# Products of ones on TensorE ahead of transposes, Gram products and the last branch's last blocks

## The chip, the cores and the metric

The kernel runs on one core of one Trainium2 chip. The metric is the device time of one execution in microseconds (us); several executions give a median. TensorE (PE in the profile) multiplies matrices into PSUM, VectorE (DVE) and ScalarE (ACT) do elementwise work, GpSimd (POOL) some of it, and SyncE (SP) issues most loads. The profile shows for every stretch the clock that TensorE was granted, as a share of full speed: 1.0 is 2.4 GHz, 0.5 is 1.2 GHz.

## The reference

One transformer block in float32, batch 1, 1024 tokens, width 1024. Two branches, an RWKV7 recurrence and a differential attention, are gated, mixed and projected; then come a mixture of 32 experts and a gated per-layer input. What the change is about is the first half:

```python
h = rms_norm(x, norm_mix[l])
proj = h @ w_in[l]
p_rwkv = proj[..., :RWKV_COLS]
p_diff = proj[..., RWKV_COLS:RWKV_COLS + DIFF_COLS]
g_rwkv, g_diff = jnp.split(proj[..., RWKV_COLS + DIFF_COLS:], 2, axis=-1)
o_rwkv = rwkv7_branch(p_rwkv, ...)      # 8 heads of 64, a scan over the tokens
o_diff = diff_attention_branch(p_diff, ...)
mixed = (jax.nn.sigmoid(g_rwkv) * (o_rwkv @ w_branch_rwkv[l])
         + jax.nn.sigmoid(g_diff) * (o_diff @ w_branch_diff[l]))
x = x + mixed @ w_out[l]
x = x + hierarchical_moe(rms_norm(x, norm_ffn[l]), ...)   # 4 groups of 8 experts, top 2
ple_gate = jax.nn.sigmoid(rms_norm(x, norm_ple[l]) @ w_ple_gate[l])
x = x + ple_gate * (p[l] @ w_ple_proj[l])
```

## The kernel before

Every large product is made of three (`mm3`, lines 69 to 71): both factors are split into a high and a low part by `split` (ACT makes the high part on line 76, DVE the low part on line 77), and three products of 512 or 256 columns are summed in PSUM.

The program runs in stages. From 0 to about 480 us: the input projection and the attention. From 480 to 703 us: the gate columns of the projection (`gates`, PSUM tile `pg8`, shown as pg) and, woven between them, `rwkv_prep` for the eight chunks of 128 tokens, c0 to c7. A chunk computes decays and keys on DVE, ACT and POOL, and then TensorE transposes 128x128 blocks into the PSUM tiles ptr (line 331): first eight of `al` and `rh` (shown as ee and ei), whose copies make AR, then eight of `be` and `ka` (shown as be and iv), whose copies make BK, in halves of four. AR, BK, LT and the rows are written to DRAM. `rwkv_inv` inverts the 32x32 blocks of four chunks in 30 serial steps on DVE (lines 400 and 402).

From 703 to 990 us: the recurrence, again chunk after chunk. `rwkv_gram` loads a chunk and makes Gram products per head (tile pG, lines 377 and 378, masked into G by DVE); `rwkv_levels` loads the inverted blocks Xd (line 414, four loads a chunk), has DVE transpose them (XT) and doubles them on TensorE (tiles pQ); `rwkv_step` makes pR, pS and pD, `rwkv_out` makes pY. Between these steps fillers run: `branch_diff` for both halves of the tokens, then one product for the per-layer input (ppp), then the RWKV branch for the first half. `branch_diff` loads four blocks of 128 rows of the attention's output (orow, line 779), transposes each (tpd, line 782), splits it (odh on ACT, odl on DVE), and calls `branch`, which makes eight blocks j of 12 products each (tile pbr) against a branch weight (braw, split to bwh and bwl) and multiplies each by a gate (bgt) on DVE (line 766 for the attention, 769 with tile btm for RWKV).

From 990 to 1030 us: the last branch, `branch(0, 1, ...)`, eight blocks of 12 products, beside the load and split of the output weight (woh, wol). Then output projection and routing up to 1165 us, the experts to 1770 us, and the last gate.

A scheduler sets the order: the program is written as generators that hand over in turns, and the framework's scheduler, with a simulated timeline, orders the instructions on each engine from that, under the dependences, the pools' buffers and the order that `issue_after` adds. An engine then works strictly through its list.

Of the kernel before, what the change touches and what calls it, by code (L numbers as in the profile page):

```python
# [22 lines left out]
F32 = mybir.dt.float32  # L23
# [29 lines left out]
class Kern:  # L53
# [13 lines left out]
    def mm3(self, ps, lh, ll, rh, rl, start, stop):  # L67
        mm = self.nc.tensor.matmul
        mm(ps, lh, rh, start=start, stop=False)  # L69
        mm(ps, lh, rl, start=False, stop=False)  # L70
        mm(ps, ll, rh, start=False, stop=stop)  # L71

    def split(self, hi, lo, src, scale=None, after=None):
        nc = self.nc
# [162 lines left out]
    def rwkv_prep(self, c):  # L237
        nc, q = self.nc, self.wq
# [7 lines left out]
        r, k, v = P[:, 0:512], P[:, 512:1024], P[:, 1024:1536]  # L246
# [14 lines left out]
        for i in range(2):  # L261
            pu = self.ps.tile([128, W], F32, name="pu", tag="s", bufs=3)
            nc.tensor.matmul(pu, lT[64 * i:64 * i + 64, 0:128], self.wa2[64 * i:64 * i + 64, :],
                             start=True, stop=True)
# [3 lines left out]
        sg, a = ua[:, 0, :], ua[:, 1, :]  # L268
# [38 lines left out]
        ka, al, rh = iv, ee, ei  # L307
# [16 lines left out]
        n = 0  # L324
        for dst, srcs in ((AR, (al, rh)), (BK, (be, ka))):
            for half in range(2):
                ps = self.ps.tile([128, 2, 2, 128], F32, name="ptr", tag="b", bufs=3)
                for pp in range(2):
                    pr = 2 * half + pp
                    for i in range(2):  # L330
                        nc.tensor.transpose(ps[:, pp, i, :], srcs[i][:, pr * 128:(pr + 1) * 128], self.ident)
                if n % 2 == 0:
                    nc.scalar.activation(dst[:, 2 * half:2 * half + 2], ps, AF.Copy)
                else:
                    nc.vector.tensor_copy(dst[:, 2 * half:2 * half + 2], ps)
                n += 1
        yield
        LT = T("LT", [128, NH, 128])
        for hb in range(2):
            ps = self.ps.tile([128, 4, 128], F32, name="pLT", tag="b", bufs=3)  # L340
            for j in range(4):
                pr, o = j, 64 * hb
# [12 lines left out]
    def rwkv_gram(self, c, R):  # L355
        nc, q = self.nc, self.wk
        T = lambda n, shape, bufs=1: q.tile(shape, F32, name=n, tag=n, bufs=bufs)
        AR = T("AR", [128, 4, 2, 128], 2)
        BK = T("BK", [128, 4, 2, 128], 1)
        nc.sync.dma_start(BK, self.sp["BK"][c])  # L360
        nc.sync.dma_start(AR, self.sp["AR"][c])
        rw = T("rows", [128, 3, W], 2)
        nc.sync.dma_start(rw, self.sp["rows"][c, :, :3])
        rw2 = T("rows2", [128, 2, W])
        nc.sync.dma_start(rw2, self.sp["rows"][c, :, 3:])
        XT = T("LT", [128, NH, 128], 1)
        nc.sync.dma_start(XT, self.sp["LT"][c])
        G = T("G", [128, NH, 3, 128], self.gb)
        R.update({nm: rw[:, i] if i < 3 else rw2[:, i - 3] for nm, i in self.spi.items()})
        R.update(AR=AR, G=G, LT=XT)  # L370
        yield
        for h in range(NH):
            if h == 4:
                yield
            pr, o = h // 2, 64 * (h % 2)
            ps = self.ps.tile([128, 3, 128], F32, name="pG", tag="s", bufs=3)
            nc.tensor.matmul(ps[:, 0, :], BK[o:o + 64, pr, 0, :], AR[o:o + 64, pr, 1, :], start=True, stop=True)
            nc.tensor.matmul(ps[:, 1:3, :], BK[o:o + 64, pr, 1, :], AR[o:o + 64, pr, :, :], start=True, stop=True)
            nc.vector.tensor_mul(G[:, h].rearrange("p a b -> p (a b)"), ps.rearrange("p a b -> p (a b)"),
                                 self.mask[:, 128:512])  # L380
        yield
# [109 lines left out]
    def rwkv_out(self, c, R):  # L491

        nc, q = self.nc, self.wk
        T = lambda n, shape, bufs=1: q.tile(shape, F32, name=n, tag=n, bufs=bufs)
        G, AR, v, sa = R["G"], R["AR"], R["v"], R["sa"]
        So = self.Sb[c % 2]
        mm = nc.tensor.matmul
        py = self.ps.tile([128, W], F32, name="pY", tag="b", bufs=3)
        for pr in range(4):
            if c:  # L500
                mm(py[:, pr * 128:(pr + 1) * 128], AR[:, pr, 1, :], So[:, pr, :], start=True, stop=False)
            for h in (2 * pr, 2 * pr + 1):
                o = slice(h * 64, h * 64 + 64)
                mm(py[:, o], G[:, h, 0, :], sa[:, o], start=not c, stop=False)
                mm(py[:, o], G[:, h, 2, :], v[:, o], start=False, stop=not c or bool(h % 2))
        yield

        h3 = lambda x: x.rearrange("p (h n) -> p h n", h=NH)
        mn = T("mn", [128, NH])
        nc.vector.tensor_reduce(mn, h3(py), axis=AX.X, op=OP.add)  # L510
        nc.vector.tensor_scalar(mn, mn, 1.0 / 64, None, op0=OP.mult)
        y = T("y", [128, W], 1)
        nc.vector.tensor_tensor(h3(y), h3(py), mn[:, :, None].to_broadcast([128, NH, 64]), op=OP.subtract)
        sq = T("wsq", [128, W])
        nc.scalar.activation(sq, y, AF.Square)
        vr = T("vr", [128, NH])
        nc.vector.tensor_reduce(vr, h3(sq), axis=AX.X, op=OP.add)
        nc.vector.tensor_scalar(vr, vr, 1.0 / 64, GN_EPS, op0=OP.mult, op1=OP.add)
        rs = self.rsqrt(q, vr, NH, "rg")
        nc.vector.tensor_tensor(h3(y), h3(y), rs[:, :, None].to_broadcast([128, NH, 64]), op=OP.mult)  # L520
        yield
        eng = nc.gpsimd if c < NT - 1 else nc.vector
        eng.tensor_tensor(y, y, self.ln_w, op=OP.mult)
        eng.tensor_tensor(y, y, R["vb"], op=OP.add)
        nc.vector.tensor_mul(y, y, R["g"])
        yield
        hi, lo = self.orT[c // 4]
        ps = self.ps.tile([128, 4, 128], F32, name="tpo", tag="b", bufs=3)
        for i in range(4):
            nc.tensor.transpose(ps[:, i, :], y[:, i * 128:(i + 1) * 128], self.ident)  # L530
        cs = slice(c % 4 * 128, c % 4 * 128 + 128)
        self.split(hi[:, :, cs], lo[:, :, cs], ps)
        if "o_r" in self.dbg:
            nc.sync.dma_start(self.dbg["o_r"][c * 128:(c + 1) * 128, :], y)
        yield
# [212 lines left out]
    def branch(self, i, half, oT, md):  # L748

        nc, q = self.nc, self.bp  # L750
        T = lambda n, shape, bufs=1, dt=F32: q.tile(shape, dt, name=n, tag=n, bufs=bufs)
        w = self.A[("w_branch_rwkv", "w_branch_diff")[i]]
        for j in range(KT):
            raw = T("braw", [128, 4, 128], 2)
            nc.sync.dma_start(raw, w[0, :, j * 128:(j + 1) * 128].rearrange("(k p) n -> p k n", p=128))
            wh = T("bwh", [128, 4, 128], 2, F32R)
            wl = T("bwl", [128, 4, 128], 2, F32R)
            self.split(wh, wl, raw)
            gt = T("bgt", [128, 512], 2)
            r = i * D + j * 128  # L760
            nc.sync.dma_start(gt, self.gd[r:r + 128, half * 512:half * 512 + 512])
            ps = self.ps.tile([128, 512], F32, name="pbr", tag="a", bufs=2)
            for k in range(4):
                self.mm3(ps, wh[:, k, :], wl[:, k, :], oT[0][:, k, :], oT[1][:, k, :], start=(k == 0), stop=(k == 3))
            if i:
                nc.vector.scalar_tensor_tensor(md[j // 4][:, j % 4, :], gt, 1.0, ps, op0=OP.add, op1=OP.mult)
            else:
                m = T("btm", [128, 512], 2)
                nc.vector.scalar_tensor_tensor(m, gt, 1.0, ps, op0=OP.add, op1=OP.mult)
                o = md[j // 4][:, j % 4, :]  # L770
                nc.gpsimd.tensor_tensor(o, o, m, op=OP.add)
            yield

    def branch_diff(self, half, pool, md):
        nc = self.nc
        oT = [pool.tile([128, 4, 512], F32R, name=f"od{z}", tag=f"od{z}", bufs=1) for z in "hl"]
        for t in range(4):
            o = self.bp.tile([128, W], F32, name="orow", tag="orow", bufs=2)
            nc.sync.dma_start(o, self.od[half * 512 + t * 128:half * 512 + (t + 1) * 128, :])
            ps = self.ps.tile([128, 4, 128], F32, name="tpd", tag="a", bufs=2)  # L780
            for i in range(4):
                nc.tensor.transpose(ps[:, i, :], o[:, i * 128:(i + 1) * 128], self.ident)
            cs = slice(t * 128, t * 128 + 128)
            self.split(oT[0][:, :, cs], oT[1][:, :, cs], ps)
            yield
        yield from self.branch(1, half, oT, md)
# [807 lines left out]
```

## Time and profile before

| | us |
|---|---|
| median of 3 runs | 1890.37 |
| lowest and highest run | 1888.12, 1900.04 |
| profiled execution | 1898.87 |
| its span, first to last instruction | 1896.8 |

In the profiled execution PE is busy 95% of the span, DVE 71%, ACT 45% and POOL 15%; the mean granted clock is 0.968. A time in the text is counted from the span's start. A timeline gives start, length, engine, line, operation, tiles and, in brackets, how long the engine sat idle before and what ended it.

### The profile page before, as it was taken

To read this page: it belongs to the slowest core of one execution; us is meant where nothing else is said; L and a number is where in the kernel's file an instruction comes from. 1 tells how busy PE (TensorE), PEld (TensorE's weight loads), DVE (VectorE), ACT (ScalarE), POOL (GpSimd) and SP (SyncE) were. 2 spreads that over 40 slices of the span, in tenths; PEclk is the share of its full clock that TensorE was granted. 3 is DMA by queue.
4 is the path that set the end of the run, shared out by engine and by line. 5 is a ranking of instruction groups with operands and counts; after the bars stand their busy time and mean duration, and the time that the engine had idled before them with its cause. 6 is when DMAs were issued, how large, how long until landed. Compare 5 with 4: busy or idle time off the path is not lost. (4 is left out here: it accounts for less than half of the span.)

```text
span 1896.8 us, 28591 instructions
## 1 busy us (share of the span) xinstructions
PE 1794.4 (95%) x10864; PEld 1489.1 (79%) x10864; DVE 1342.8 (71%) x2580; ACT 858.1 (45%) x1241; POOL 275.7 (15%) x209
## 2 busy tenths in 40 slices
PE   6999999999998989999998996999999999999698
PEld 6999899898776776888876885888777777777487
DVE  6455867743777947766756668898878788888773
ACT  5244444421333322122223225777677777777431
POOL 0311201000222220010303001122111111110000
PEclk9999999999997998889998997999999999999799
DMA  6432242337576567444535557999999999999641
GB/s 219 129 117 78 79 134 79 100 112 251 192 254 228 186 206 247 141 137 158 172 110 191 176 180 254 370 367 376 328 344 356 369 357 357 348 348 354 261 176 45
DMA packets 241789, 421.39 MB, mean 222 GB/s; under 512 B 38769, under 2 KB 115697, under 8 KB 240754
## 3 DMA queue, kind: packets, MB, share of 16 engines
q1 hardware_dynamic: 194546, 346.12, 53.4%
q10 hardware_dynamic: 37888, 56.64, 8.2%
q0 software_dynamic: 9216, 16.80, 2.4%
q8 instruction: 86, 1.41, 0.3%
q14 instruction: 53, 0.43, 0.1%
HBM read 346.07 MB, written 90.18 MB: 230 GB/s over the span
## 5 line engine op out<-in xcount | busy, mean ns | idle before, releaser
L77 DVE TENSOR_TENSOR ewl<-ewp,ewh 128x2048 fp32r<-128x2048 f32 x108 | 245.6, 2286 | 38.1 <-ACT ewh L76 34.8
L69 PE MATMUL pj<-whi,hh 128*128 128x256 f32 x832 | 239.7, 288 | 0.0
L70 PE MATMUL pj<-wlo,hh 128*128 128x256 f32 x832 | 239.2, 288 | 0.3 <-DVE wlo L77 0.3
L71 PE MATMUL pj<-whi,hl 128*128 128x256 f32 x832 | 237.4, 286 | 0.0
L76 ACT ACTIVATE ewh<-ewp 128x2048 fp32r<-128x2048 f32 x108 | 204.5, 1912 | 18.3 <-PE pg L1163 8.5
L77 DVE TENSOR_TENSOR ewl<-md,ewh 128x2048 fp32r<-128x2048 f32 x84 | 191.2, 2286 | 28.0 <-ACT ewh L76 26.1
L69 PEld LDWEIGHTS pj<-whi,hh 128*128 128x128 f32 x832 | 159.2, 191 | 7.2 <-issue 6.6
L70 PEld LDWEIGHTS pj<-wlo,hh 128*128 128x128 f32 x832 | 159.2, 191 | 6.5 <-issue 5.3
L76 ACT ACTIVATE ewh<-md 128x2048 fp32r<-128x2048 f32 x84 | 159.3, 1910 | 9.6 <-PE pg L1163 4.2
L71 PEld LDWEIGHTS pj<-whi,hl 128*128 128x128 f32 x832 | 159.0, 191 | 2.6 <-issue 2.3
L1073 POOL DMA_INDIRECT xg<-h2d,ids x32 | 64.4, 2012 | 409.8 <-PE ptp L1063 390.5
L69 PE MATMUL pg<-hh,whi 128*128 128x512 f32 x256 | 105.7, 413 | 0.0
L70 PE MATMUL pg<-hl,whi 128*128 128x512 f32 x256 | 104.6, 409 | 0.0
L1163 PE MATMUL pu<-ewh,exh 128*128 128x512 f32 x256 | 103.5, 404 | 0.0
L71 PE MATMUL pg<-hh,wlo 128*128 128x512 f32 x256 | 103.1, 403 | 0.0
L1163 PE MATMUL pg<-ewh,exh 128*128 128x512 f32 x256 | 102.7, 401 | 0.0
L1163 PE MATMUL pg<-ewh,exl 128*128 128x512 f32 x256 | 102.3, 400 | 0.2 <-DVE exl L77 0.2
L1163 PE MATMUL pu<-ewh,exl 128*128 128x512 f32 x256 | 101.4, 396 | 0.0
L1116 PE MATMUL pey<-ewh,eal 128*128 128x512 f32 x256 | 97.7, 401 | 2.7 <-DVE eal L77 2.7
L1116 PE MATMUL pey<-ewh,eah 128*128 128x512 f32 x256 | 97.9, 402 | 1.4 <-ACT eah L76 1.4
L76 ACT ACTIVATE whi<-wraw 128x1024 fp32r<-128x1024 f32 x42 | 44.5, 1060 | 113.9 <-DMA wraw<-in_w_in_dram 56.4
L77 DVE TENSOR_TENSOR wlo<-wraw,whi 128x1024 fp32r<-128x1024 f32 x42 | 55.0, 1309 | 41.5 <-ACT whi L76 41.4
(457 smaller groups left out, 4262.6 us busy)
## 6 DMA issues: line engine op xcount, KB each, us to landing
ewp<-in_w_down_dram SPq DMA_DIRECT2D x42, 1024.0 KB, 7.7
ewp<-in_w_gate_dram SPq DMA_DIRECT2D x33, 1024.0 KB, 7.9
ewp<-in_w_up_dram SPq DMA_DIRECT2D x33, 1024.0 KB, 8.3
md<-in_w_up_dram SPq DMA_DIRECT2D x31, 1024.0 KB, 8.7
md<-in_w_gate_dram SPq DMA_DIRECT2D x31, 1024.0 KB, 7.6
md<-in_w_down_dram SPq DMA_DIRECT2D x22, 1024.0 KB, 7.4
wraw<-in_w_in_dram SPq DMA_DIRECT2D x42, 512.0 KB, 3.9
gd<-pjev ACTq DMA_DIRECT2D x32, 256.0 KB, 4.5
```

The lines of the kernel that those rows point to most:

```text
L69: mm(ps, lh, rh, start=start, stop=False)
L70: mm(ps, lh, rl, start=False, stop=False)
L71: mm(ps, ll, rh, start=False, stop=stop)
L76: a = nc.scalar.activation(hi, src, AF.Copy)
L77: b = nc.vector.tensor_tensor(lo, src, hi.bitcast(F32), op=OP.subtract)
L1073: self.lastx = self.nc.gpsimd.indirect_dma_start(out=xg, out_offset=None, in_=self.h2d, in_offset=bass.IndirectOffsetOnAxis(ap=tid, axis=0 ...
L1116: mm(self.pey[b], a[z][:, k + i, :], hi[:, i, half(b)], start=(k + i + z == 0), stop=False)
L1163: mm(P[i], x[z][:, k0 + j, :], hi[:, j, :], start=(k0 + j + z == 0), stop=False)
```

## The change

`mm3` returns its last product. A new method `warm(ps, n, after)` issues n products of a 128x128 block of ones with ones broadcast to 512 columns into a PSUM tile that the next real products overwrite, each ordered after the instruction `after` on the same engine, without a semaphore. They stand at four places: in `rwkv_prep` of chunks c3 to c6 ahead of the first be/iv transposes (7 each); in `rwkv_gram` of chunks c1 to c7 ahead of the first head (6 each, after the last pY product, and pG now fills 512 columns of which 384 are used); in `branch_diff` ahead of blocks t=1 and t=2 of the first half and t=2 of the second (9 each); and in the last branch ahead of j=5, 6 and 7 (5, 5 and 10).

```diff
-        mm(ps, ll, rh, start=False, stop=stop)
+        return mm(ps, ll, rh, start=False, stop=stop)
+
+    def warm(self, ps, n, after):
+
+        for _ in range(n):
+            m = self.nc.tensor.matmul(ps, self.ones, self.ones[:, None, :].to_broadcast([128, 4, 128]),
+                                      start=True, stop=True)
+            self.issue_after(m, after)
...
                 ps = self.ps.tile([128, 2, 2, 128], F32, name="ptr", tag="b", bufs=3)
+                if n == 2 and 3 <= c <= 6:
+                    self.warm(ps.rearrange("p a b n -> p (a b n)"), 7, tr)
...
-                        nc.tensor.transpose(ps[:, pp, i, :], srcs[i][:, pr * 128:(pr + 1) * 128], self.ident)
+                        tr = nc.tensor.transpose(ps[:, pp, i, :], srcs[i][:, pr * 128:(pr + 1) * 128], self.ident)
...
-            ps = self.ps.tile([128, 3, 128], F32, name="pG", tag="s", bufs=3)
+            ps = self.ps.tile([128, 512], F32, name="pG", tag="s", bufs=3)
+            if h == 0 and c:
+                self.warm(ps, 6, self.lastpe)
+            ps = ps[:, :384].rearrange("p (a n) -> p a n", a=3)
...
-                mm(py[:, o], G[:, h, 2, :], v[:, o], start=False, stop=not c or bool(h % 2))
+                self.lastpe = mm(py[:, o], G[:, h, 2, :], v[:, o], start=False, stop=not c or bool(h % 2))
...
+            if not i and half and j >= 5:
+                self.warm(ps, (5, 5, 10)[j - 5], self.lastpe)
             for k in range(4):
-                self.mm3(ps, wh[:, k, :], wl[:, k, :], oT[0][:, k, :], oT[1][:, k, :], start=(k == 0), stop=(k == 3))
+                self.lastpe = self.mm3(ps, wh[:, k, :], wl[:, k, :], oT[0][:, k, :], oT[1][:, k, :],
+                                       start=(k == 0), stop=(k == 3))
...
+            if (t == 1 or t == 2) and not half or t == 2:
+                self.warm(ps.rearrange("p a n -> p (a n)"), 9, tr)
             for i in range(4):
-                nc.tensor.transpose(ps[:, i, :], o[:, i * 128:(i + 1) * 128], self.ident)
+                tr = nc.tensor.transpose(ps[:, i, :], o[:, i * 128:(i + 1) * 128], self.ident)
```

The scheduler's order changes with it. Line numbers behind `warm` grow by 7 to 17, so line 331 is 340 after the change, 377 is 389, 779 is 794, 782 is 799; the products of ones are line 76. The first place is TensorE at the be/iv transposes of chunk c4; before:

```order
L331 MATMUL ptr<-ident,ei 128x128
L331 MATMUL ptr<-ident,be 128x128
L331 MATMUL ptr<-ident,iv 128x128
L331 MATMUL ptr<-ident,be 128x128
L331 MATMUL ptr<-ident,iv 128x128
L71 MATMUL pg_6962<-hh_109,wlo 128x512
L69 MATMUL pg_6962<-hh_109,whi 128x512
L70 MATMUL pg_6962<-hl_111,whi 128x512
L71 MATMUL pg_6962<-hh_109,wlo 128x512
L276 MATMUL pc<-ua,tmat 128x512
```

The same place after the change, where pg are gate products and pc is a product of the next chunk's decays:

```order
L340 MATMUL ptr<-ident,ei 128x128
L76 MATMUL ptr<-ones 128x512 x7
L340 MATMUL ptr<-ident,be 128x128
L340 MATMUL ptr<-ident,iv 128x128
L340 MATMUL ptr<-ident,be 128x128
L340 MATMUL ptr<-ident,iv 128x128
L283 MATMUL pc<-ua,tmat 128x512
```

Seven products of ones came in, and four gate products moved behind pc. At c6 thirteen gate products stood between the first be and the first iv transpose, and none does now; behind the last chunk 81 stand ahead of tpd, and 53 before.

The second place is TensorE at the start of the recurrence, from the last gate product on; before:

```order
L71 MATMUL pg_7318<-hh_109,wlo 128x512
L782 MATMUL tpd<-ident,orow 128x128 x16
L69 MATMUL pbr<-odh,bwh 128x512
L70 MATMUL pbr<-odl,bwh 128x512
L71 MATMUL pbr<-odh,bwl 128x512
```

And after the change, up to the transposes of the fourth block of rows:

```order
L71 MATMUL pg_7346<-hh_109,wlo 128x512
L799 MATMUL tpd<-ident,orow 128x128 x4
L76 MATMUL tpd<-ones 128x512 x9
L799 MATMUL tpd<-ident,orow 128x128 x4
L76 MATMUL tpd<-ones 128x512 x9
L799 MATMUL tpd<-ident,orow 128x128 x4
...
L434 MATMUL pQ<-Xd_7407,LT 32x32 x15
L799 MATMUL tpd<-ident,orow 128x128 x2
L389 MATMUL pG<-AR,BK 128x128
L390 MATMUL pG<-AR,BK 128x256
L799 MATMUL tpd<-ident,orow 128x128 x2
```

The fourth group of transposes moved behind Gram products and the first pQ, and the first pbr product behind it and behind the next 32 pQ products; up to these 32 pQ, 65 pbr products stood there before.

The third place is SP's list of loads at the same time; before:

```order
L779 DMA orow<-od 128x512
L755 DMA braw<-in_w_branch_diff_dram 128x4x128
L779 DMA orow<-od 128x512
L221 DMA ln_w<-in_rwkv_ln_w_dram 128x512
L360 DMA BK<-spBK 128x1024
L361 DMA AR<-spAR 128x1024
L363 DMA rows<-sprows 128x1536
L365 DMA rows_7391<-sprows 128x1024
L367 DMA LT<-spLT 128x1024
L390 DMA inv<-ld 128x1024
L414 DMA Xd_7379<-xd 32x8x32 x4
```

After the change:

```order
L794 DMA orow<-od 128x512
L228 DMA ln_w<-in_rwkv_ln_w_dram 128x512
L369 DMA BK<-spBK 128x1024
L370 DMA AR<-spAR 128x1024
L372 DMA rows<-sprows 128x1536
L374 DMA rows_7419<-sprows 128x1024
L376 DMA LT<-spLT 128x1024
L402 DMA inv<-ld 128x1024
L426 DMA Xd_7407<-xd 32x8x32 x4
L794 DMA orow<-od 128x512
```

The fourth orow load moved behind the chunk's loads and the four Xd loads. On DVE, its odl split moved behind the XT transposes and the inversion step of 192 columns. In the last branch the list of TensorE is 60 products, 5 of ones, 12, 5 of ones, 12, 10 of ones, 12; two of the products of j=4 stood ahead of j=5 before and ten among or behind its products, and all twelve stand ahead of it now.

## Rows read from the trace of the kernel before

**Rows 1.** Busy time by engine, clock, DMA in the two stages with the recurrence.

```profile
480.00:703.00 223.00, 213.71 (x1021) 160.83 (x1020) 171.40 (x337) 68.71 (x119) 61.52 (x45) 0.95 0.64 213
703.00:990.00 287.00, 273.78 (x2476) 227.12 (x2475) 187.24 (x445) 64.72 (x130) 32.61 (x25) 0.92 0.51 161
```

**Rows 2.** Windows, PE alone: length, PE busy (products), PE clock, DMA share, GB/s.

```profile
572.00:576.00 4.00, 3.60 (x11) 0.58 1.00 344
599.00:617.00 18.00, 17.33 (x48) 0.53 0.52 193
708.00:716.00 8.00, 4.91 (x14) 0.57 0.98 343
729.00:733.00 4.00, 4.00 (x12) 0.58 0.62 181
756.00:764.00 8.00, 8.00 (x72) 0.57 0.28 81
797.00:815.00 18.00, 18.00 (x140) 0.53 0.43 136
851.00:863.00 12.00, 12.00 (x74) 0.57 0.40 113
1002.00:1006.00 4.00, 4.00 (x11) 0.57 1.04 391
1012.00:1020.00 8.00, 6.63 (x17) 0.57 0.33 98
```

**Rows 3.** Timeline of PE: start, length, line, operation, tile, idle before.

```profile
541.58 0.39 PE L71 MATMUL pg<-hh,wlo 128*128 128x512 f32 x1
541.80 0.40 PE L69 MATMUL pg<-hh,whi 128*128 128x512 f32 x1
...
605.12 0.63 PE L69 MATMUL pg<-hh,whi 128*128 128x512 f32 x1
605.55 0.63 PE L70 MATMUL pg<-hl,whi 128*128 128x512 f32 x1
```

**Rows 4.** Timeline of PE: waits at the be/iv transposes of chunks c3, c4, c6.

```profile
572.40 0.48 PE L331 MATMUL ptr<-ident,iv 128*128 128x128 f32 x1 [2.48 <-DVE iv L308]
...
598.03 0.33 PE L331 MATMUL ptr<-ident,iv 128*128 128x128 f32 x1 [1.79 <-DVE iv L308]
...
658.14 0.33 PE L331 MATMUL ptr<-ident,be 128*128 128x128 f32 x1 [1.28 <-DVE be L306]
...
662.35 0.33 PE L331 MATMUL ptr<-ident,iv 128*128 128x128 f32 x1 [0.92 <-DVE iv L308]
```

**Rows 5.** Timeline of PE: waits at tpd and Gram products in the recurrence.

```profile
707.12 0.63 PE L782 MATMUL tpd<-ident,orow 128*128 128x128 f32 x4 [1.90 <-DMA orow<-od]
...
710.40 1.08 PE L782 MATMUL tpd<-ident,orow 128*128 128x128 f32 x4 [2.66 <-DMA orow<-od]
...
754.83 0.63 PE L782 MATMUL tpd<-ident,orow 128*128 128x128 f32 x4 [2.15 <-DMA orow<-od]
...
795.97 0.48 PE L377 MATMUL pG<-AR,BK 64*128 64x128 f32 x2 [1.21 <-DVE G L379]
```

**Rows 6.** Windows of tile pbr alone: PE, PEld and DVE busy, clock, DMA.

```profile
703.00:739.40 36.40, 18.93 (x64) 13.97 (x65) 3.21 (x5) 0.86 0.82 265
```

**Rows 7.** Timeline of SP, the queue that issues loads.

```profile
710.75 5.56 SPq L414 DMA_DIRECT2D Xd<-xd  x4
```

**Rows 8.** DMA issues: count, KB each, median us to landing.

```profile
orow<-od SPq DMA_DIRECT2D x8, 256.0 KB, 4.5
```

**Rows 9.** Timeline of DVE at the start of the recurrence.

```profile
732.32 0.69 DVE L77 TENSOR_TENSOR bwl<-braw,bwh 128x512 fp32r<-128x512 f32 x1
733.04 0.44 DVE L415 STREAM_TRANSPOSE XT<-Xd 32x256 f32<-32x256 f32 x1
733.50 0.36 DVE L400 TENSOR_TENSOR Xt<-inv 128x192 f32<-128x192 f32 x1
```

**Rows 10.** Timeline of PE in the last branch.

```profile
1013.37 0.76 PE L69 MATMUL pbr<-or1h,bwh 128*128 128x512 f32 x1 [3.23 <-DVE btm L769]
```

**Rows 11.** Timeline of DVE in the last branch.

```profile
1013.15 2.36 DVE L77 TENSOR_TENSOR bwl<-braw,bwh 128x512 fp32r<-128x512 f32 x2
```

## The prediction

> **What bounds the kernel now.** I read the windows by stage first. In the two stages that hold the recurrence (480 to 703 us: gates and preparation of the chunks; 703 to 990 us: the recurrence itself with branch products as fillers) PE is busy 213.71 of 223 and 273.78 of 287 us, and DVE 171.40 and 187.24 [rows 1]. TensorE is the bound, and what the change can win must come from PE's idle time or from the clock at which it works. The reader should see the last columns: the granted clock is 0.95 and 0.92 of full speed there, although PE hardly idles.
>
> Windows of a few us place the loss: nine stretches at 0.53 to 0.58, so nearly wholly at the lower of the two levels, 1.2 GHz of 2.4 [rows 2]. Two kinds of work stand ahead of them: waits at transposes (those that end at 572.40 and 598.03 [rows 4], at 707.12, 710.40 and 754.83 [rows 5], the one that ends at 1013.37 [rows 10]), and, at 797, long rows of small products after a wait of only 1.21 us [rows 5], while PE counts as busy for all of 18.00 us [rows 2].
>
> The excess of a stretch is its length times one minus its clock, times its busy share. In the order of [rows 2]: 1.5, 8.1, 2.1, 1.7, 3.4, 8.5, 5.2, 1.7 and 2.9, together **35.1 us**. That is all that a better clock can give back here, 1.9% of the span.
>
> The Trainium skill ("TensorE: Matmul & The Clock Gate", Part 1) says that for modelling the ramp penalty is under 1% of a typical kernel span. The rows here show 1.9%, so it doesn't hold for this kernel. By it no more than 19 us would be there to win, and the sum below, which takes 26.7, would come out 8 us higher.
>
> **The price of one product.** A product with 512 columns goes out 0.22 to 0.23 us after the one before it at full clock (541.58, 541.80) and 0.43 us at the lower level (605.12, 605.55) [rows 3]; I take 0.2275. The products of ones have that size. There are 28 + 42 + 27 + 20 = 117 of them, 26.6 us if nothing hides them. PE works in order, so they are free only where PE would wait anyway for what stands behind them.
>
> **Place 1, the transposes of chunks c3 to c6** (28 products, 6.4 us). Seven products, 1.6 us, stand between the AR and the be/iv transposes. In c3 and c4 the iv transpose waits 2.48 and 1.79 us for DVE, in c6 the be transpose 1.28 and iv 0.92 [rows 4]: a group is hidden in each of these three, 4.8 us. At c5 PE doesn't wait, and 1.6 us is paid. But the scheduler takes gate products out from between the transposes: at c4 the four ahead of pc are gone, at c6 the thirteen between be and iv, and behind the last chunk stand 81 gate products in front of tpd instead of 53. Those 28 products covered waits of DVE, whose times don't change. I charge all of them, 28 x 0.2275 = 6.4 us; the other bound is 0, if they cover other waits. Against that stand the stretches at 572 and 599, 1.5 + 8.1 = 9.6 us, which follow just these waits; I credit both. Sum 6.4 - 4.8 + 6.4 - 9.6 = **-1.6 us**.
>
> **Place 3, first half, and the start of the recurrence** (18 products, 4.1 us). Nine stand ahead of the second and nine ahead of the third group of tpd transposes, where PE waits 1.90 us for orow, and 2.66 us for the fourth [rows 5]: hidden. What I fear there is the order. The load of the fourth orow now stands on SP behind the four Xd loads. Those hold SP from 710.75 for 5.56 us [rows 7]; from 716.3 an orow takes 4.5 us to land [rows 8], so its transposes start at about 721 instead of 710.40. Its odl split on DVE stands behind the XT transposes and the inversion step of 192 columns, which are at 733.04 and 733.50 now; four operations of the pbr blocks (two bwl splits at 0.69 us [rows 9], and two md of like size) no longer stand ahead of it, so it comes at 731 to 734. PE then starts pbr there, and no longer at 712. Up to 739.4 there are 64 pbr products [rows 6], 14.6 us of work at full clock, which must now be done afterwards; what else stands there is done earlier. From a start at 731 that ends at 745.6, from 734 at 748.6, against 739.4: 6.2 to 9.2 us, less about 1 us for the 32 pQ products that now stand ahead. I take **+7 us**; the lower bound is 0, if orow and odl come no later than now. The stretches at 708 and 729 come from this start and are not credited.
>
> **Place 2, the Gram products** (42 products, 9.6 us). Six stand before the first head of each chunk from c1 on, behind the last pY product. The one wait nearby is 1.21 us, for G [rows 5], and it is at a later head, so I hide nothing (bound: 1.2). The stretches at 756, 797 and 851 follow such Gram products; I credit all three, 3.4 + 8.5 + 5.2 = 17.1 us. Sum **-7.5 us**. This is the least certain term: at 797 PE was busy without a gap and still lost the clock, with 140 products in the stretch. If six products ahead of the same row don't change that, the term is +9.6.
>
> **Place 3, second half** (9 products, 2.05 us): the wait of 2.15 us at 754.83 [rows 5] covers them, **0**; bound 2.05 if the wait has moved.
>
> **Place 4, the last blocks** (20 products, 4.6 us). The first five stand ahead of the block j=5. The wait of 3.23 us that ends at 1013.37 [rows 10] falls in front of the ten remaining products of j=4, since these now stand ahead of j=5 and wait for the bwl split that DVE starts at 1013.15 [rows 11] and that takes 0.69 us by the row of its like [rows 9]. So the ones come behind the wait and behind the fall of the clock at 1012. The stretches at 1002 and 1012 (4.6 us) stay, and all 20 products lie on the path, with 0.5 us for the split that is waited for: **+5 us**. Behind, PE is the bound again, and the shift isn't made up.
>
> **Sum**: -1.6 + 7 - 7.5 + 0 + 5 = **+2.9 us**. The rows are of an execution of 1898.87 us (span 1896.8), 8.5 above the median of the runs shown, 1890.37; the difference goes on that median: **1893 us**. Nothing behind the last branch is touched.
>
> **Rivals.** *A, everything is got back.* The start of the recurrence costs nothing, the scheduler's displaced products cover other waits, and all nine stretches go, those at 1002 and 1012 by another arrival. Then 35.1 us against 26.6 - 4.8 - 4.1 - 2.05 = 15.6: -19.5, **1871 us**. For it speaks that low clock is visible where the products are put; against it that the last branch's products come after the falls, and that SP's order is plain. *B, slower: the recurrence's small products keep the clock down.* Six large products ahead of a row of small ones delay the fall, and it comes within that row as now. Then the 17.1 us stay: +2.9 + 17.1 = +20, **1910 us**; it decides from the point where less than 10 of the 26.7 us that I credit come back. If place 1 fails too, 1920. For it speaks the 797 stretch, busy 18.00 of 18.00 at 0.53 [rows 2]; against it that of the seven chunks with such rows only three lost the clock [rows 2]. *C, the start is harmless*: orow comes in time, the term of 7 goes, **1886 us**, still no measurable change.
>
> The skill's same page, Part 4, says that transposes don't count as PE work in the way that products do. Place 1 fits that. Place 2 has few transposes and fell all the same, so the rule doesn't reach it; if only transposes caused falls, the Gram products would win nothing and B would be the result, 1910.
>
> **How the numbers follow.** One per cent is 19 us, about what a measurement of this kernel can tell from no change. Forecast with C 0.58, A and what lies beyond it 0.17, B and beyond 0.25. The range must leave out no more than 0.2: from A's 1871 to just beyond B, whose tail to 1920 I leave out in part: 1870 to 1912. The two unknowns that make it so wide are the recurrence's clock (17.1 us) and the start (0 to 9).
>
> **What would show it.** Right: granted clock 1.0 at 570 to 617 and from 790 to 860, PE idle for some 10 us or more between tpd and the first pbr, that pbr at 731 to 734, low clock still at the last branch and that stage some 5 us longer. Wrong: a first pbr before 722 (no late orow), low clock in the recurrence (B), or DVE waits that leave PE idle in the preparation beyond 6 us. A fall of the clock at places that had none before would break the sum altogether, since I move no falls, only remove them.

## The result and the profile after

The changed kernel takes 1910.29 us (median of 5 executions, 1907.85 to 1913.78), the kernel before 1890.37; the ratio is 1.0093 with a 95% interval of 1.0072 to 1.0114. In a second set it was 1.0085 (1.0060 to 1.0110). It is slower by a little under one per cent. The profiled execution took 1907.85 us with a span of 1905.5, and that of before 1898.87: their difference is 9.0 us, not 20, and that is the first thing to explain. The mean granted clock rose from 0.968 to 0.978.

Milestones, from the first and last starts of tiles in the two traces: the first tpd product moved from 703.4 to 706.1, the first pbr from 712.2 to 731.4, the recurrence's last tpo from 991.0 to 995.9, the last product of the last branch from 1026.4 to 1035.6, the first product of the experts from 1163.0 to 1172.2. Behind that little differs: the end is 8.7 us later.

The windows by stage of the changed kernel, which answer to [rows 1]:

```profile
480.00:703.00 223.00, 212.18 (x1036) 160.48 (x1036) 170.60 (x339) 68.72 (x120) 60.28 (x45) 0.98 0.65 216
703.00:990.00 287.00, 280.83 (x2540) 229.75 (x2539) 185.39 (x433) 61.69 (x124) 32.70 (x26) 0.96 0.49 157
```

The clock is 0.98 and 0.96 where it was 0.95 and 0.92, and PE in the recurrence is busy 280.83 us where it was 273.78. The windows of low clock (length, PE busy, clock, DMA), which answer to [rows 2], the last row for the recurrence behind its start:

```profile
579.00:588.00 9.00, 7.49 (x31) 0.62 0.77 277
599.00:617.00 18.00, 18.00 (x94) 1.00 0.52 186
654.00:660.00 6.00, 4.82 (x17) 0.72 0.83 266
716.00:738.00 22.00, 20.09 (x159) 0.53 0.66 223
797.00:815.00 18.00, 17.97 (x129) 1.00 0.58 190
851.00:863.00 12.00, 12.00 (x110) 1.00 0.10 29
1006.00:1011.00 5.00, 5.00 (x15) 0.66 1.05 390
1016.00:1024.00 8.00, 6.25 (x15) 0.57 0.32 98
740.00:990.00 250.00, 249.00 (x2314) 1.00 0.47 148
```

The stretches at 599, 797 and 851 are at full clock. Others stand at 579, 654 and, longest, at 716 to 738, and the last branch has its two. The one at 579 goes with a wait that the kernel before doesn't have: PE waits 2.78 us for BK ahead of pLT products (LT of a chunk).

```profile
580.51 1.23 PE L352 MATMUL pLT<-AR,BK 64*128 64x128 f32 x8 [2.78 <-ACT BK L342]
```

The waits of PE at the be/iv transposes (timeline; in brackets the idle time before), which answer to [rows 4]:

```profile
571.11 0.33 PE L340 MATMUL ptr<-ident,iv 128*128 128x128 f32 x1 [0.86 <-DVE iv L315]
...
653.24 0.33 PE L340 MATMUL ptr<-ident,be 128*128 128x128 f32 x1 [1.84 <-DVE be L313]
...
655.18 0.48 PE L340 MATMUL ptr<-ident,iv 128*128 128x128 f32 x1 [1.60 <-DVE iv L315]
```

At c3 0.86 us is left of 2.48. At c6 the two waits were 1.28 and 0.92 us and are now 1.84 and 1.60, although seven products stand in front of them: the gate products that the scheduler took away had covered more. The start of the recurrence on PE:

```profile
711.67 0.60 PE L799 MATMUL tpd<-ident,orow 128*128 128x128 f32 x4
...
715.28 0.50 PE L389 MATMUL pG<-AR,BK 64*128 64x128 f32 x4 [3.01 <-DMA AR<-spAR]
```

The third group of tpd ends and PE waits 3.01 us for AR. The two waits for orow at the start, in [rows 5], are gone; PE waits for AR and, at 722.28, 1.91 us for Xd in their place. SP at the same time, which answers to [rows 7]:

```profile
710.73 4.83 SPq L426 DMA_DIRECT2D Xd<-xd  x4
717.11 0.62 SPq L794 DMA_DIRECT2D orow<-od  x1
```

The fourth orow goes out at 717.11, behind the four Xd. DVE's fourth odl split, and the first pbr product:

```profile
729.85 0.68 DVE L84 TENSOR_TENSOR odl<-tpd,odh 128x512 fp32r<-128x512 f32 x1
```

```profile
731.40 0.80 PE L69 MATMUL pbr<-odh,bwh 128*128 128x512 f32 x1
```

The split ends at 730.53, and the product stands without idle time behind a row of pQ products that runs from 730.39: when it starts, it doesn't wait for the split.

Last, TensorE in the last branch and the products of ones by tile (duration minimum, median, maximum; first and last start), which answer to [rows 10] and [rows 3]:

```profile
1017.75 0.79 PE L71 MATMUL pbr<-or1h,bwl 128*128 128x512 f32 x1 [3.74 <-DVE bwl L84]
...
1022.18 2.04 PE L76 MATMUL pbr<-ones 128*128 128x512 f32 x5
```

```profile
L76 PE MATMUL pG<-ones x42: 387/397/505, 745.3 to 944.3; 128*128 128x512 f32 x42
L76 PE MATMUL ptr<-ones x28: 387/395/481, 568.3 to 651.0; 128*128 128x512 f32 x28
L76 PE MATMUL tpd<-ones x27: 387/397/497, 706.9 to 799.0; 128*128 128x512 f32 x27
L76 PE MATMUL pbr<-ones x20: 387/394/629, 1022.2 to 1032.8; 128*128 128x512 f32 x20
```

The wait of 3.74 us is for the bwl split, and the first products of ones come 4.4 us behind it. These five take 2.04 us, 0.41 each: they still run at the lower level.

### The profile page after: what moved, and what is told of

It reads as the page before. It is cut to its first block, busy times and chain, and to the rows that moved or that the text cites. A ratio compares the mean times of both kernels' runs of the same rounds, so it can differ in the third digit from the quotient of the medians.

```text
span 1905.5 us, 28816 instructions
## 1 busy us (share of the span) xinstructions
PE 1806.1 (95%) x10981; PEld 1496.2 (79%) x10981; DVE 1343.8 (71%) x2580; ACT 857.7 (45%) x1241; POOL 273.8 (14%) x209
## 5 line engine op out<-in xcount | busy, mean ns | idle before, releaser
L83 ACT ACTIVATE ewh<-md 128x2048 fp32r<-128x2048 f32 x84 | 159.2, 1910 | 9.7 <-PE pg L1180 4.3
L1182 PE MATMUL pg<-ewl,exh 128*128 128x512 f32 x256 | 72.1, 403 | 12.3 <-DVE ewl L84 12.2
```

Of the source, the lines that this page charges most:

```text
L83: a = nc.scalar.activation(hi, src, AF.Copy)
L1182: mm(P[i], x[0][:, k0 + j, :], lo[:, j, :], start=False, stop=(k0 + j == KT - 1))
```

## How the executions were compared

Each result lists span and mean granted clock of every execution. I split a span in two: the **loss**, (1 - clock) x span, and the **rest**, clock x span. Over 80 executions of the kernel before, all of 81 but the longest (1910.84 us), the loss has a mean of 49.6 us and a standard deviation of 5.6 us, the rest 1840.0 and 2.3. So most of what differs from one execution of the same program to another is the clock. The loss counts idle time at a low clock too: in the profiled execution of before it is 61 us, of which 44 are PE's work. Differences between kernels are what it is for. The means of 5 to 12 executions are good to about 1 us in the rest and 1 to 2 us in the loss.

The table has the mean loss and rest as differences from before, and the ratio. From one trace of each kernel come the time from the first to the last product of the experts' tile pu and what the clock loses in it. The last column is the rest without the experts: the difference in the rest less the difference of the experts' time without its loss (before: 600.9 - 1.2 = 599.7).

| kernel | executions | ratio to before | loss | rest | experts, of it loss | rest without experts |
|---|---|---|---|---|---|---|
| before | 80 | | 49.6 | 1840.0 | 600.9, 1.2 | |
| before_again | 12 | 1.0009 (0.9987 to 1.0032) | +2.3 | -0.4 | 600.1, 0.5 | -0.3 |
| changed | 5 | 1.0093 (1.0072 to 1.0114) | -7.2 | +25.8 | 600.2, 0.5 | +25.8 |
| after_again | 6 | 1.0085 (1.0060 to 1.0110) | -11.2 | +27.1 | 601.3, 1.9 | +27.4 |
| place1_alone | 12 | 0.9981 (0.9961 to 1.0000) | -7.1 | +4.9 | 600.4, 1.0 | +5.2 |
| place2_alone | 12 | 1.0048 (1.0029 to 1.0066) | -3.7 | +12.9 | 610.5, 4.4 | +6.5 |
| place3_alone | 12 | 0.9983 (0.9964 to 1.0001) | -5.6 | +2.1 | 598.3, 1.1 | +4.6 |
| place4_alone | 12 | 1.0002 (0.9979 to 1.0025) | +0.4 | +1.4 | 598.6, 1.6 | +4.1 |
| places_1_and_2 | 6 | 1.0103 (1.0065 to 1.0142) | -5.4 | +24.2 | 612.6, 4.1 | +15.4 |
| places_1_and_3 | 6 | 1.0104 (1.0072 to 1.0137) | -0.6 | +19.3 | 612.9, 4.4 | +10.5 |
| places_1_2_3 | 12 | 1.0057 (1.0034 to 1.0080) | -10.6 | +21.2 | 601.0, 1.2 | +21.1 |
| places_1_2_4 | 6 | 1.0122 (1.0096 to 1.0148) | -7.8 | +30.4 | 612.0, 3.5 | +21.6 |
| all_tiny | 12 | 1.0037 (1.0019 to 1.0054) | -3.9 | +10.2 | 600.8, 1.0 | +10.1 |
| one_chunk | 12 | 0.9995 (0.9979 to 1.0012) | -1.6 | +1.3 | 598.3, 0.9 | +3.6 |

## The experiments

### Each place alone

Each kernel is the changed one with three of the four calls of `warm` taken out. The calls are, in the order of the text, those of place 1, 2, 3 and 4:

```diff
+                if n == 2 and 3 <= c <= 6:
+                    self.warm(ps.rearrange("p a b n -> p (a b n)"), 7, tr)
+            if h == 0 and c:
+                self.warm(ps, 6, self.lastpe)
+            if (t == 1 or t == 2) and not half or t == 2:
+                self.warm(ps.rearrange("p a n -> p (a n)"), 9, tr)
+            if not i and half and j >= 5:
+                self.warm(ps, (5, 5, 10)[j - 5], self.lastpe)
```

> Only the 28 products ahead of the be/iv transposes. Theory S (the sum by places holds, the missing 17 us of the median lie in the recurrence and the start): -1.6 us by the prediction, +2.7 us by the first tpd of the changed kernel (706.1 against 703.4). Theory V (the profiled execution of the kernel before had more low clock than its ordinary ones, so that the products give back less than the rows promised): +4 to +8 us.

Ratio 0.9981: loss -7.1, rest +4.9, together -2.2 us. The time agrees with S (-1.6), the reason doesn't. S has a low clock taken away in the preparation; by windows of 1 us the clock loses 5.1 us from 560 to 703 in this trace, and 10.2 and 5.1 in two traces of the kernel before (the second is before_again, below). It is the recurrence, from 740 to 990, that loses less, 3.4 us against 17.1 and 11.9, and no product of ones stands there.

> Only the 42 products ahead of the Gram products. S: -7.5 us (9.6 paid, 17.1 got back). V: +5 to +9.6 us, since ordinary executions of the kernel before lose the clock less in the recurrence. Rival B (small products keep the clock down) would show the falls at 797 and 852 still there, and +9.6.

Ratio 1.0048, +9 us, as V has it, but the trace has another reason. In the recurrence the clock is whole:

```profile
740.00:990.00 250.00, 245.24 (x2394) 1.00 0.49 155
```

That refutes rival B. The +9 stand in the experts, whose code is the same: pu takes 610.5 us from first to last, and 600.9 before. Without them place 2 is at +6.5 in the rest and -6.9 in the loss, so near no change: neither S nor V. The longest waits of PE in that stage (line and tile, releaser, us in total, times, longest), here and in the changed kernel:

```profile
PE pg L1174 <- ACT ewh L83: 8.5, 7, 2.0
PE pey L1127 <- DVE eal L84: 7.0, 6, 2.5
PE pey L1127 <- ACT eah L83: 6.0, 8, 1.6
```

```profile
PE pg L1182 <- DVE ewl L84: 12.2, 17, 0.8
PE pey L1133 <- DVE eal L84: 2.7, 2, 1.7
PE pey L1133 <- ACT eah L83: 0.7, 1, 0.7
```

The scheduler ordered the experts' splits otherwise. Of the 436 instructions that ACT runs from the first pu product on, 219 stand at another place than in the kernel before, and 6 in the changed kernel. PE idles 21.5 us in that stage, 16.5 before, and the clock loses 4.4 there, 1.2 before. All fourteen traces go by this order: where 0 to 6 of ACT's instructions are displaced, pu takes 600.1 to 601.3 us (seven traces), with 32 it takes 598.3 to 598.6 (place3_alone, place4_alone, one_chunk), and with 184 to 219 it takes 610.5 to 612.9 (place2_alone, places_1_and_2, places_1_and_3, places_1_2_4). Why the scheduler takes one or the other, no run shows.

> Only the 27 products among the tpd transposes, with the late fourth orow on SP. S: +7 us, PE idle and at low clock from 712 to 737, first pbr behind 728. V: the same, +5 to +10; if the order at the start is harmless, 0 to +2.

Ratio 0.9983, -3.5 us in the means: neither. The first pbr is at 726.9 us, so the late start is there, and the clock is low at the start; then the recurrence stays at nearly full clock, without one product ahead of a Gram product, though nine products of ones stand at 791 among the second half's tpd (windows of 700 to 740 and of the recurrence behind it):

```profile
700.00:740.00 40.00, 34.40 (x251) 0.74 0.75 242
740.00:990.00 250.00, 244.83 (x2282) 0.99 0.49 155
```

Of the 3.5 us, 2.6 are in the experts (598.3 against 600.9).

> Only the 20 products in the last branch; the order of everything else is that of the kernel before. Both theories: +4.5 to +5 us, the last branch 9 us longer at most; falls at 1002 and 1012 as before.

Ratio 1.0002, with an interval of 4 us on either side, so the +4.5 is not resolved by it; the rest without the experts, +4.1, agrees. In the trace the last branch lasts 37.4 us from its first to its last product and 34.1 before, the experts 2.3 us less. The trace has one fall there, at 1008, and not both; so has that of places_1_and_2, at 1010, without a product of ones in the last branch.

### Places together

> Places 1 and 3 without 2 and 4. Each run's span is split in what the clock loses, (1 - mean clock) x span, and the rest. Alone, place 1 changed the loss by -7.0 and the rest by +4.9, place 3 by -5.5 and +2.1. If losses add (theory A): -5.5 us against before. If the products take the same falls away, and the loss has a floor near that of the whole change (theory F, loss never much below 42 us): rest +7, loss -7, so 0.

+19 to +20 us, and neither A nor F. The experts explain most: 612.9 us, 12.0 more than before, of which 3.2 are loss. Without them the rest is +10.5, where both theories had +7, and the loss about -4, where A had -12.5 and F -7.

> Places 1 and 2 without 3 and 4; the fourth orow stands early on SP, as before. A: rest +17.8, loss -10.6, so +7 us. F: rest +17.8, loss -7, so +11. If only the late orow makes the changed kernel slow, this one is at -4 to 0.

Ratio 1.0103, rest +24.2, of which 8.8 are in the experts (612.6 us). What remains, +15.4, is more than the two places alone have there (5.2 + 6.5). Both theories had +17.8 only because they counted the experts' part of place2_alone as the price of its products. Without the experts the loss is about -8, so this kernel stands at +7, not at -4 to 0: the late orow is not all that makes the changed kernel slow.

> The change without the last branch's products. A: rest +19.9, loss -16, so +4 us. F: rest +20 to +24, loss -7, so +13 to +17, that is 2 to 5 us under the whole change.

Ratio 1.0057: the rest of +21.2 is F's, the loss of -10.6 is between the two, and so is the time, +11 us. The experts are those of before. Against the changed kernel's two sets (+25.8 and +27.1) the rest is 4.6 and 5.9 lower; place 4's 20 products at 0.2275 make 4.55 us, and +5 was predicted.

> The change without the products among the tpd transposes; the fourth orow goes out early, as before, but the experts' splits on ACT and DVE stand in the order of places_1_and_2, which ran that stage in 610 us and not 598. If the tpd products and their order cost 7 us in the front: 1160 to 1165 us for the first expert product (changed kernel 1172), and +12 behind it, so +15 to +20 in all. If tpd is not what costs: first expert product at 1170 or later, +25 to +30.

First product of the experts at 1162.8 us, as expected if tpd is what costs; in all 1.0122, +23 us, above the 15 to 20 expected, with the experts at 612.0. The rest without the experts is +21.6, against +25.8 and +27.4 in the two sets of the changed kernel: the tpd products and the order that they bring cost **4 to 6 us** of rest beside the other places. The clock comes on top: by windows of 1 us PE's work from 703 to 740 us loses 5.2 here, and 9.3 and 7.5 in the two traces of the changed kernel.

### Columns

The changed kernel with products of 8 columns, same number and same order rules:

```diff
-            m = self.nc.tensor.matmul(ps, self.ones, self.ones[:, None, :].to_broadcast([128, 4, 128]),
+            m = self.nc.tensor.matmul(ps[:, 0:8], self.ones, self.ones[:, 0:8],
```

> All four places with the same number of products, each with 8 columns in place of 512: next to no time on PE (117 x some 30 ns), little that could hold the clock. If the columns keep the clock up (A and F): loss as before, near 49, rest +0 to +4, time within 0.2% or a few us slower. If the cost is in the order that the added instructions bring (theory R), the rest goes up by 10 us or more with hardly any product in it.

Rest +10.2, loss -3.9, where A and F had at most +4 and none. The price of 30 ns was wrong: seven go in 0.78 us, 0.11 us each, as long as a transpose (timeline of PE):

```profile
567.74 0.27 PE L340 MATMUL ptr<-ident,ee 128*128 128x128 f32 x1
567.85 0.27 PE L340 MATMUL ptr<-ident,ei 128*128 128x128 f32 x1
567.88 0.92 PE L76 MATMUL ptr<-ones 128*128 128x8 f32 x7
568.66 0.33 PE L340 MATMUL ptr<-ident,be 128*128 128x128 f32 x1
```

So 117 of them are 12.9 us of PE, half of the 26.6, and the rest is +10.2 against +25.8: that fits PE's time for the products. With hardly a column in the products, the recurrence stays at nearly full clock in this trace:

```profile
740.00:990.00 250.00, 246.89 (x2342) 0.99 0.49 155
```

Theory R had just this rest, +10 or more. It isn't needed, and isn't excluded: the scheduler's order is not that of the changed kernel (all sixteen tpd stand together, the fourth orow goes out early).

### The same kernels again, and a candidate

> The kernel before, unchanged, with a profile of another execution. Theory V (the rows of the prediction came from an execution with more low clock than usual): the stretches are fewer or shorter, some at other places, and 10 to 17 us less of PE's work at the low level than the 35.1 of the prediction's rows. If falls belong to places of the program, the same nine stretches appear, 35 us.

The time is that of before. The windows of this second execution of the same program, the last row for the recurrence:

```profile
599.00:617.00 18.00, 17.09 (x83) 1.00 0.58 206
627.00:635.00 8.00, 6.21 (x17) 0.57 0.70 276
723.00:735.00 12.00, 12.00 (x70) 0.57 0.44 126
797.00:817.00 20.00, 20.00 (x149) 0.57 0.38 122
851.00:863.00 12.00, 12.00 (x105) 1.00 0.45 127
740.00:990.00 250.00, 242.44 (x2330) 0.95 0.47 148
```

The stretch at 599, 8.1 us in the sum, is at full clock, and so is that at 851, 5.2 us; one stands at 627 that wasn't there. The seven others are there again, those at 572, 708, 756, 1002 and 1012 at 573, 706, 757, 999 and 1010. PE's work at the low level loses 27.4 us by windows of 1 us up to 1140 us, and 35.2 in the first: 7.8 less, between the two forecasts. The profiled execution had a loss of (1 - 0.968) x 1896.8 = 60.7 us, the mean of 80 is 49.6.

Full clock at 599 doesn't win all of the 8.1 us. PE comes earlier to the transposes of c5 and waits there for DVE, where the first trace shows no wait, and the fall at 627 begins there:

```profile
628.79 0.47 PE L331 MATMUL ptr<-ident,be 128*128 128x128 f32 x1 [3.09 <-DVE be L306]
```

The first tpd product comes 2.8 us earlier, at 700.6. So it is in other traces without products at place 1: place2_alone has the long fall at 599 and no such wait, place3_alone and place4_alone have not the long fall and wait 3.10 and 3.09 us.

> The changed kernel, unchanged, with another profile and on the same chip as the next two. The fall behind the late orow at 716 to 737 is there again if PE's idle time makes it; the others may move. Time +16 to +20 us against before.

Ratio 1.0085, +16 us, as expected. The fall is there again, at 719 to 737, with first pbr at 733.1; so are those at 579, 658, 1006 and 1016. In the two traces of the changed kernel the falls keep their places. The wait of 2.6 to 2.8 us for BK and a fall between 579 and 589 stand in all seven traces that have the products of place 1 in full, and in none of the seven others; no trace with these products has a fall at 599.

> Only the seven products at chunk c4, whose wait of 1.79 us hides them. The experts' order is that of place3_alone and place4_alone, which ran the stage in 596 us, 2 us less than before. Candidate for a version that beats both kernels: 2 to 5 us under before, if the order of the experts carries it -2.2 by itself.

```diff
-                if n == 2 and 3 <= c <= 6:
+                if n == 2 and c == 4:
```

Ratio 0.9995 (0.9979 to 1.0012): no gain. The experts give 2.6 us in the trace, and the rest without them is +3.6, though the wait was to hide the seven products. It hid only a part. Of the 1.79 us at the iv transpose 1.17 are left, and PE waits 1.76 us ahead of pc, where it waited 0.67 before: the gate products that stood ahead of pc now stand behind it.

```profile
600.54 1.12 PE L283 MATMUL pc<-ua,tmat 128*128 128x512 f32 x2 [1.76 <-DVE ua L274]
```

No version here clearly beats the kernel before; place1_alone and place3_alone come nearest, with intervals that end at 1.0000 and 1.0001.

## Why the prediction was right, and which step failed

The time, 1910.3, lies in the range, 2 us from its end, and the forecast "within 1%" held, at its upper edge; the sum was 17 us too low. The sum was near in what PE must do and wrong in what the clock gives back. That the range reached so far was due to rival B, whose mechanism is refuted: that the number was right is in good part luck.

**The price of the products and of the order** (the sum without the clock: 6.4 - 4.8 + 6.4 + 7 + 9.6 + 5 = 29.6 us). Measured as the rest: +25.8 and +27.1. Right as a total, less so by places: place 1 predicted +8.0, 5.2 alone; place 2 predicted +9.6, 6.5 alone without the experts and 10.2 beside place 1 (15.4 - 5.2); the start with place 3 predicted +7, 4.6 alone and 4 to 6 beside the others; place 4 predicted +5, 4.1 alone and 4.6 to 5.9 beside the others. The four alone make 5.2 + 6.5 + 4.6 + 4.1 = 20.4, against 25.8 and 27.4 together. What alone is hidden isn't all hidden together; which wait was used twice, no run shows. The nine products of place 3's second half were to cost nothing; in the trace of the changed kernel they go out at 797.03 without a wait beside them, so the bound of 2.05 us holds there.

**The details of the start.** The orow issue came at 717.11 (forecast 716.3), the transposes of the fourth group at 725.06 (721), odl at 729.85 (731 to 734), the first pbr at 731.40 (731 to 734). The last number is right by another way: PE was to idle for 10 us or more and wait for the split, but it idled 25.40 - 20.23 = 5.2 us between 706 and 731.4, for AR, Xd and, 0.25 us, ACT, worked at a low clock, and came to pbr behind the pQ products without idle time.

**The last branch** held: the wait moved to bwl, and the products came after the clock had fallen, so that they took neither fall away in the changed kernel.

**The clock is the step that failed.** I credited 26.7 us: 9.6 at place 1 and 17.1 at place 2. The loss fell by 7.2 (11.2 in the second set). Of the 19.5 us that are missing, 11.1 are the choice of the execution: the rows came from one that had lost 60.7 us, against a mean of 49.6. In the sum the median stood for the time and the profiled execution for the loss, and the step from one to the other, 8.5 us in time, was mentioned and not taken off the credit. Where the others are, the traces show; PE's work at the low level loses, by windows of 1 us, in us:

| stretch | credited | before, before_again | changed, after_again |
|---|---|---|---|
| 560 to 703, preparation | 9.6 | 9.7, 4.4 | 4.8, 4.4 |
| 703 to 740, start of the recurrence | 0 | 3.8, 7.8 | 9.3, 7.5 |
| 740 to 990, recurrence | 17.1 | 17.1, 11.9 | 0, 0 |
| 990 to 1040, last branch | 0 | 4.6, 3.2 | 4.7, 4.3 |

The credit of place 1 failed. The prediction said "I move no falls, only remove them", but the order moved them: the new wait of 2.78 us at 580.51 comes with a fall, and another fall stands at 654. That the gate products which the scheduler took away had covered the new wait is likely, and not tested by itself. And its largest part, 8.1 us at 599, was not there to be won in full: in the second execution of before, at full clock, a wait of 3.09 us comes in its place. So the sign "granted clock 1.0 at 570 to 617" came but for 579 to 588.

At the start the change lengthens the fall or leaves it: 700 to 740 is at 0.74 and 0.79 in the changed kernel, at 0.87 and 0.79 in the kernel before, whose second trace has a fall at 723 to 735 too. In the five traces with the late orow PE's work loses 7.4 to 9.4 us there, in the nine others 2.3 to 7.8.

The credit of place 2 held in these traces. The recurrence from 740 to 990 is at 1.00 in all six traces with it, at 0.93 to 0.95 in before, before_again, place4_alone and one_chunk. But it is at 0.98 to 0.99 without it in place1_alone, place3_alone, places_1_and_3 and all_tiny. The last three have other products there, nine of ones among tpd or the 42 with 8 columns; place1_alone has none, and only the order differs. How much of the credit needs the 42 products, one trace of each kernel doesn't show.

The Trainium skill's tip in "TensorE: Matmul & The Clock Gate", Part 1, that the ramp penalty is under 1% of a span, is on a kernel's first products; the prediction took it as a bound on all low clock. As such a bound it is not borne out by the mean loss, 49.6 us of 1889.6, 2.6%, nor by PE's work alone, 44 us in the profiled execution, 2.3%. Its credit of at most 19 us would have come nearer than mine, by a bound that doesn't hold.

**Rival B** had the time, 1910, and not the mechanism: its falls within the small products of the recurrence are gone. **Rival A** and **C** are out: the products and the order cost 26 us of rest, and the fourth orow came late. What I hadn't among the rivals is that added products reorder the experts, some 140 us behind the last product of ones, at 10 to 12 us. The changed kernel escapes it, and four of its parts don't. What sets which of the orders the scheduler takes stays open.

## What to carry to other kernels

A low clock in one trace is in part a draw: of nine stretches, seven were there in a second execution of the same program and two, half of the credit, were not. Before a gain is credited to a place, compare a second execution, and take the loss as (1 - clock) x span over all executions. Ask also what stands behind a stretch at low clock: where PE would wait for another engine, full clock gives back only a part. A product that nobody reads costs its full issue time unless the wait behind it is sure to stay, and work that it pushes away uncovers other waits. Under a scheduler that works from a simulated timeline, look at the order of stages far behind the edit: here an unchanged stage moved by up to 12 us, more than any place of the change.

## What was unexpected in the hardware

A product with 8 columns takes 0.11 us of PE in a row of its like, half of one with 512 columns (0.2275), and as long as a transpose with 128 (0.11 in the same timeline). In the trace each of the seven has a load of 128x128 weights of its own, and these too go out every 0.11 us (0.86 us for seven from 567.86); the pQ products with 32x32 weights go faster, 30 in 1.05 us at 724.08 in the changed kernel. So few columns buy little here; whether the load of the weights sets the pace, no run separates. And executions of one program without any change differ by 20 us (1881.34 to 1901.62 in before_again) with a rest that has a standard deviation of 2.8 us: most of that difference lies in the clock.
